# A decoder layer on one core: start loads in quarters, merge residuals from PSUM, residual scaling moved to the down projection

## The chip, the cores and the metric

The kernel runs on one core of a Trainium2 chip. The metric is the device time of one execution in microseconds (us), the median of several runs. The engines are named as the profile names them: PE (TensorE, matrix products; PEld is its weight load), DVE (VectorE), ACT (ScalarE), POOL (GpSimd) and SP (SyncE, which here only issues transfers).

## The reference, cut to what matters

One layer of a hybrid decoder on 544 rows (512 of a prompt and 8 sequences of 4) with 1024 channels and a feed-forward width of 2816. In the code below, attention, the convolution and the caches are left out.

```python
def token_mixers(u, mw, slopes, conv_prev, kv_prev):
    a = u @ w_in + b_in
    glu = a[..., :CONV_CH] * jax.nn.sigmoid(a[..., CONV_CH:QKV_OFF])
    qkv = a[..., QKV_OFF:GATE_OFF].reshape(B, T, 3, N_GROUPS, N_SLOTS, HEAD_DIM)
    gate_c = jax.nn.sigmoid(a[..., GATE_OFF:GATE_OFF + D_MODEL])
    gate_a = jax.nn.sigmoid(a[..., GATE_OFF + D_MODEL:])
    ...
    y_conv = conv_branch(conv_in, w_dw, b_dw, conv_ln_g, conv_ln_b, w_pc, b_pc)
    ...
    y_att = o.reshape(B, T, ATT_WIDTH) @ w_pa + b_pa
    y = (gate_c * y_conv + gate_a * y_att) @ w_out + b_out
    return y, new_kv, new_conv

def block(x, c, lw, slopes, conv_prev, kv_prev):
    ...
    mod = (jax.nn.silu(c) @ w_ada + b_ada)[:, None, :]
    sh1, sc1, g1, sh2, sc2, g2 = jnp.split(mod, 6, axis=-1)
    u = x * (1 + sc1) + sh1
    y, new_kv, new_conv = token_mixers(u, ..., slopes, conv_prev, kv_prev)
    x = layer_norm(DN_ALPHA * x + (1 + g1) * y, ln1_g, ln1_b)
    u = x * (1 + sc2) + sh2
    h = (jax.nn.silu(u @ w_gate) * (u @ w_up)) @ w_down
    x = layer_norm(DN_ALPHA * x + (1 + g2) * h, ln2_g, ln2_b)
    return x, new_kv, new_conv
```

## The kernel before, in words

All activations lie transposed, channels on the 128 partitions and rows along the free dimension, in two halves of 272 columns: h = 0 holds prompt rows 0 to 271, h = 1 the other 240 and the 32 sample rows. Each float32 product is made of three products of a rounded high part and a low residual (high by high, high by low, low by high). So an operand has to be prepared: ACT casts it to the high part (L133, L828, L962) and DVE subtracts that from the original to get the residual (L134, L829, L952).

Weights come in blocks of 1024 x 128 through a stream: `load_more` issues loads on SP's queue into four buffers (`wr`), `prep_to(n)` prepares blocks up to number n, and `w_next` prepares up to three ahead and returns one. A buffer is loaded anew only when its block is prepared. `mm_group` (L199, L200, L202) multiplies one block with both halves: 48 products of 272 columns for eight row tiles. On PE, ACT, DVE and POOL the instructions run in the order in which the program writes them; background work is cut into generators that `tick` advances between groups of products.

**Start.** The modulation vector's first third is made in four groups g: `ada_mm(g)` is 32 products with a 2 MB weight tile `ga[g]` (64 entries in the trace), and `make_u(g)` copies the result, transposes it on PE, makes `modT` on DVE (it needs the `vec` load) and from it the rows of tiles 2g and 2g + 1 of the modulated input `U`. The first three blocks of the input projection accumulate as tiles come (`early_mm(g)`, 36 products each); the loop from the fourth block on uses `mm_group`. The other two thirds of the modulation run between later blocks (`ada_gen`), from eight 2 MB loads (`ada_load`) on POOL's queue.

**Merge and output projection.** For each of eight channel tiles the attention projection is added on POOL (L845) to the gated convolution branch, and `merge_split` makes the operand rows `M`. The output projection (weights `wo`) then takes half 0 for all eight blocks, and half 1 after it. `z` is loaded again with the input rows, scaled by ALPHA with a bias on POOL (L989), and takes each block's result. `Stats` gathers the sums for the layer norm: a running sum on DVE (L881), squares on ACT (L873) added on POOL (L882), each turned into column sums by PE with a matrix of ones (L924, L925); `finish` makes the mean and the deviation. `ln1_gen(h)` normalizes and makes the feed-forward input `u2[h]`; for half 0 it also keeps its float32 rows in `TF` (L976), during half 1's projection.

**Feed-forward.** Gate and up blocks run in three chunks. Blocks 0 to 3 run classically, blocks 4 to 20 by `seven`: seven products of half-size operands in place of eight, with sums of weights made on POOL (L1077) and sums of rows (`T`) made from `tf` on DVE (L1262 to L1267). In the first chunk `keep` multiplies the rows of `z` by ALPHA and the norm's gain (L1258), a few rows at a time between the blocks. The chunk ends with a down projection whose results are added to `z`.

## Time and profile before

| | us |
|---|---|
| median of 3 runs | 1032.31 |
| lowest, highest | 1032.12, 1032.55 |
| profiled execution | 1033.35 |
| its span | 1031.6 |
| mean granted clock of PE in it | 0.986 of full speed |

A row of a timeline gives the start and the duration of one instruction, or of a run of equal ones (xN, with their time together), and in brackets how long the engine stood idle before it and what ended that. Tables of stretches give the busy time of each engine in a stretch, with the instructions that touch it. The granted clock is 1.00 at 2.4 GHz and 0.50 at 1.2 GHz.

### The profile page before, as it was taken

Reading aid. Unit: us, or ns where it says so; the run is one execution under the profiler, and the core shown is the slowest. Engines: PE = TensorE matmul, PEld = TensorE weight load, DVE = VectorE, ACT = ScalarE, POOL = GpSimd, SP = SyncE. Lnnn points to the kernel's source line nnn. Section 1 sums busy time; section 2 is a strip of 40 time slices with the busy share of each in tenths; the row PEclk is TensorE's granted clock in tenths of the full one; section 3 lists DMA queues with packets and bytes.
Section 4 is the critical chain, followed back from the end, with each engine's and each line's share of the span. In section 5 each row is a group of like instructions: output and inputs, shape, how many; then the busy total and the mean of one; then the engine's idle time right before and its main releaser. Section 6 shows DMA issues by size and latency. Waiting matters only on the chain.

```text
span 1031.6 us, 21539 instructions
## 1 busy us (share of the span) xinstructions
PE 985.8 (96%) x8964; PEld 942.2 (91%) x8964; DVE 652.1 (63%) x1156; ACT 479.7 (47%) x931; POOL 236.3 (23%) x279
## 2 busy tenths in 40 slices
PE   4999999999999999999999998989999999999995
PEld 3887999999998999999999998989999999999994
DVE  3422788879886654342217887687546875578687
ACT  3312235545447667534433445656325652266333
POOL 0301010010013310101103444054014440344046
PEclk8999999999999999999999998999999999999998
DMA  9998687696784674699953620124964769565612
GB/s 379 361 385 319 244 298 261 246 339 233 277 324 163 238 271 154 236 378 384 367 202 99 242 83 21 42 83 170 349 255 162 266 209 360 205 246 207 213 50 86
DMA packets 44945, 242.64 MB, mean 235 GB/s; under 512 B 7408, under 2 KB 10736, under 8 KB 37680
## 3 DMA queue, kind: packets, MB, share of 16 engines
q1 hardware_dynamic: 34592, 126.83, 34.4%
q10 hardware_dynamic: 7632, 88.43, 23.0%
q0 software_dynamic: 2624, 26.02, 6.3%
q8 instruction: 70, 1.15, 0.4%
q14 instruction: 27, 0.22, 0.1%
HBM read 231.36 MB, written 97.58 MB: 319 GB/s over the span
## 4 chain that ended last, share of the span: by engine, by line
PE 61%; DVE 12%; issue 8%; ACT 7%; POOL 6%; DMA 5%; ACTq 0%; DVEq 0%; POOLq 0%
PE mm L199 15%; PE mm L200 14%; PE mm L202 14%; POOL ss L1077 4%; DMA wr<-in_w_gu 3%; PE od L740 2%; PE mm L1120 2%; PE Sd L705 2%; PE mm L1121 2%; PE mm L1122 2%; PE adaps L334 1%; DVE mrg L829 1%; DMA wr<-in_w_in 1%; PE pt L516 1%; DVE wl L134 1%
## 5 line engine op out<-in xcount | busy, mean ns | idle before, releaser
L199 PE MATMUL mm<-u,wh 128*128 128x272 f32 x1016 | 283.4, 296 | 1.2 <-ACT wh L133 0.9
L200 PE MATMUL mm<-u,wh 128*128 128x272 f32 x1016 | 275.6, 289 | 0.0
L202 PE MATMUL mm<-u,wl 128*128 128x272 f32 x1016 | 213.2, 290 | 1.3 <-DVE wl L134 1.2
L199 PEld LDWEIGHTS mm<-u,wh 128*128 128x128 f32 x1016 | 192.4, 189 | 15.8 <-issue 11.4
L200 PEld LDWEIGHTS mm<-u,wh 128*128 128x128 f32 x1016 | 192.7, 190 | 0.3
L134 DVE TENSOR_TENSOR wl<-wr,wh 128x1024 fp32r<-128x1024 f32 (+2 forms) x100 | 117.5, 1176 | 86.5 <-ACT wh L133 86.5
L202 PEld LDWEIGHTS mm<-u,wl 128*128 128x128 f32 x1016 | 160.4, 189 | 1.9 <-DVE wl L134 1.9
L133 ACT CAST wh<-wr 128x1024 fp32r<-128x1024 f32 (+2 forms) x100 | 97.0, 972 | 64.6 <-PE mm L200 50.5
L439 DVE SCALAR_TENSOR_TENSOR convy<-glu,vec,convy 128x512 f32<-128x512 f32 x120 | 95.7, 797 | 2.5
L1077 POOL TENSOR_TENSOR ss<-wr 128x512 f32<-128x512 f32 x34 | 50.6, 1487 | 189.3 <-DVE s L1104 85.9
L200 PE MATMUL mm<-h,wh 128*128 128x272 f32 x240 | 64.7, 288 | 0.0
L199 PE MATMUL mm<-h,wh 128*128 128x272 f32 x240 | 64.5, 286 | 0.0
L1034 DVE SCALAR_TENSOR_TENSOR z<-mm,modT,z 128x272 f32<-128x272 f32 (+1 forms) x48 | 21.7, 479 | 49.0 <-PE mm L202 49.0
L637 ACT ACTIVATE qk<-mm,vec 128x272 f32<-128x272 f32 (+1 forms) x48 | 25.9, 627 | 56.5 <-PE mm L202 56.5
L202 PE MATMUL mm<-h,wl 128*128 128x272 f32 x240 | 49.6, 288 | 0.0
L1093 ACT CAST wh<-ss 128x512 fp32r<-128x512 f32 (+1 forms) x34 | 28.4, 835 | 42.8 <-POOL ss L1077 32.1
L199 PEld LDWEIGHTS mm<-h,wh 128*128 128x128 f32 x240 | 45.2, 188 | 0.0
L200 PEld LDWEIGHTS mm<-h,wh 128*128 128x128 f32 x240 | 45.1, 188 | 0.0
L1120 PE MATMUL mm<-ta,wh 128*128 128x272 f32 x136 | 40.4, 297 | 4.6 <-DVE wg L1142 4.6
L509 ACT ACTIVATE P<-P,st 128x256 f32<-128x256 f32 x64 | 31.2, 488 | 28.2 <-DVE st L503 25.7
L654 POOL DMA_DIRECT2D out_kv<-qk x4 | 2.4, 597 | 182.5 <-ACT qk L637 182.5
L200 PE MATMUL mm<-mrg,wo 128*128 128x272 f32 x128 | 37.8, 296 | 1.8 <-DVE mrg L829 1.7
(329 smaller groups left out, 2545.4 us busy)
## 6 DMA issues: line engine op xcount, KB each, us to landing
out_s<-in_c ACTq DMA_DIRECT2D x32, 2044.0 KB, 10.4
wr<-in_w_in SPq DMA_DIRECT2D x60, 512.0 KB, 6.6
wr<-in_w_gu SPq DMA_DIRECT2D x44, 512.0 KB, 3.8
KT<-in_kt SPq DMA_DIRECT2D x24, 792.0 KB, 7.9
VV<-in_vv SPq DMA_DIRECT2D x24, 768.0 KB, 7.8
gb<-in_w_ada POOLq DMA_DIRECT2D x8, 2048.0 KB, 16.9
out_s<-in_c ACTq DMA_DIRECT2D x8, 2032.0 KB, 10.1
ga<-in_w_ada SPq DMA_DIRECT2D x8, 1024.0 KB, 14.3
```

The source lines that it names most:

```text
L133: act.copy(out=hv, in_=raw)
L134: dve.tensor_tensor(out=lv, in0=raw, in1=hv.bitcast(F32), op=ALU.subtract)
L199: pe.matmul(ps[h][:, :HC], lhsT=hi[:, k], rhs=A[h][:, 0, k], start=(k == 0), stop=False)
L200: pe.matmul(ps[h][:, :HC], lhsT=hi[:, k], rhs=A[h][:, 1, k], start=False, stop=False)
L202: pe.matmul(ps[h][:, :HC], lhsT=lo[:, k], rhs=A[h][:, 0, k], start=False, stop=(k == nk - 1))
L439: dve.scalar_tensor_tensor(out=o, in0=src, scalar=sc, in1=o, op0=ALU.mult, op1=ALU.add)
L509: act.activation(out=p[:, a:b], in_=p[:, a:b], func=AF.Exp, bias=st[:, kd, s, hh, 0:1], accum_out=st[:, kd, s, hh, 1:2])
L637: act.activation(out=o, in_=src, func=AF.Identity, bias=V("b_in", col))
L1034: dve.scalar_tensor_tensor(out=zz[:, :n1], in0=ps[:, :n1], scalar=modT[:, 5, m, 0:1], in1=zz[:, :n1], op0=ALU.mult, op1=ALU.add)
L1077: pool.tensor_tensor(out=o, in0=x, in1=y, op=op)
L1093: act.copy(out=hi, in_=src_of(f, n))
L1120: pe.matmul(ps[:, :HC], lhsT=hi[:, k], rhs=B[:, 0, k], start=(first and k == 0), stop=False, skip_group_check=not first)
```

## The change

At the start, the x tiles and the first three weight blocks are loaded in quarters, one set behind each modulation group, and prepared in quarters (`prep_quarters`). The products of the first three blocks are spread differently over the groups, and 18 products of a matrix of ones (`warm`) are added. The large constant load and four of the modulation loads are issued on SP's queue in place of ACT's and POOL's. In the merge, ACT copies the high part to PSUM as well, and the residual reads that copy in seven of eight tiles. The first two output blocks run interleaved, rows 0 to 5 of both ahead of rows 6 and 7. ACT in place of POOL scales `z`. `finish` writes POOL's additions first and the reciprocal ahead of the second pair. The float32 rows of `u2[0]` are made in the feed-forward start (`again`) in place of the second half's projection, and the second up block is prepared there. `keep` moves to the first chunk's down projection.

```diff
@@ -214,16 +214,26 @@
     act.dma_start(out=vec, in_=I["vec"])
-    ga = []
-    for g in range(4):
-        t = big_tile(3 + g, [128, 8, 512], F32, f"ga{g}")
+    ga = [big_tile(3 + g, [128, 8, 512], F32, f"ga{g}") for g in range(4)]
+
+    def ga_load(g):
         for i in range(2):
-            sp.dma_start(out=t[:, 4 * i:4 * i + 4], in_=I["w_ada0"][g, :, 4 * i:4 * i + 4])
-        if g % 2 == 0:
-            sp.dma_start(out=x_sb[:, 2 * g:2 * g + 4], in_=I["x_t"][:, 2 * g:2 * g + 4])
-        if g < 2:
-            load_more(1 + 2 * g)
-        ga.append(t)
+            sp.dma_start(out=ga[g][:, 4 * i:4 * i + 4], in_=I["w_ada0"][g, :, 4 * i:4 * i + 4])
+
+    def x_load(g):
+        sp.dma_start(out=x_sb[:, 2 * g:2 * g + 2], in_=I["x_t"][:, 2 * g:2 * g + 2])
+
+    def w_quarters(g):
+        for m in range(NE):
+            sp.dma_start(out=eraw[m][:, 2 * g:2 * g + 2], in_=stream[m][0][:, 2 * g:2 * g + 2])
+
+    NE = 3
+    eraw = [wrp.tile([128, 8, 128], F32, tag="wr", name="wr") for _ in range(NE)]
+    for g in range(4):
+        ga_load(g)
+        x_load(g)
+        w_quarters(g)
+    pos.update(load=NE, prep=NE, use=NE)
     load_more()
-    act.dma_start(out=cst[:, 128:], in_=I["cst"][:, 128:])
-    dve.memset(cpad, 0.0)
+    sp.dma_start(out=cst[:, 128:], in_=I["cst"][:, 128:])
     dve.memset(ones, 1.0)
+    dve.memset(cpad, 0.0)
     dve.memset(epst, EPS)
@@ -282,9 +292,23 @@
 
-    NE = 3
     early = [[(pmm if m < 2 else ps_s).tile([128, 512], F32, tag="mm" if m < 2 else "s", name="mm") for _ in range(2)] for m in range(NE)]
-    ew = []
 
-    def early_mm(g):
+    def warm(n):
+        t = ps_t.tile([128, 128], F32, tag="t", name="warm")
+        for _ in range(n):
+            pe.matmul(t, lhsT=ones, rhs=ones, start=True, stop=True)
+
+    ew = [(whp.tile([128, 8, 128], F32R, tag="wh", name="wh"), wlp.tile([128, 8, 128], F32R, tag="wl", name="wl")) for _ in range(NE)]
+
+    def prep_quarters(g):
+        ks = slice(2 * g, 2 * g + 2)
         for m in range(NE):
             hi, lo = ew[m]
+            act.copy(out=hi[:, ks], in_=eraw[m][:, ks])
+            dve.tensor_tensor(out=lo[:, ks], in0=eraw[m][:, ks], in1=hi[:, ks].bitcast(F32), op=ALU.subtract)
+            done[m] = g == 3
+        load_more()
+
+    def early_mm(g, ms=range(NE)):
+        for m in ms:
+            hi, lo = ew[m]
             for k in (2 * g, 2 * g + 1):
@@ -297,19 +321,18 @@
 
-    a0 = ada_mm(0)
-    make_u(0, a0)
-    prep_to(1)
-    a1 = ada_mm(1)
-    prep_to(2)
-    make_u(1, a1)
-    prep_to(3)
-    for m in range(NE):
-        ew.append(preps.pop(m))
-    pos["use"] = NE
-    early_mm(0)
-    a2 = ada_mm(2)
-    make_u(2, a2)
-    early_mm(1)
-    a3 = ada_mm(3)
-    make_u(3, a3)
-    early_mm(2)
+    warm(12)
+    make_u(0, ada_mm(0))
+    prep_quarters(0)
+    warm(6)
+    early_mm(0, (0, 1))
+    make_u(1, ada_mm(1))
+    prep_quarters(1)
+    early_mm(0, (2,))
+    early_mm(1, (0,))
+    make_u(2, ada_mm(2))
+    prep_quarters(2)
+    early_mm(1, (1, 2))
+    early_mm(2, (0,))
+    make_u(3, ada_mm(3))
+    prep_quarters(3)
+    early_mm(2, (1, 2))
     dve.tensor_scalar(out=qb, in0=V("b_in", 0, 60), scalar1=0.125, scalar2=None, op0=ALU.mult)
@@ -320,5 +343,5 @@
 
-    def ada_load(c):
+    def ada_load(c, eng=pool):
         t = big_tile(aslots[c], [128, 2, 2048], F32, f"gb{c}")
-        pool.dma_start(out=t, in_=I["w_ada12"][c])
+        eng.dma_start(out=t, in_=I["w_ada12"][c])
         abox[c] = t
@@ -364,4 +387,4 @@
     ctmp = glu[:, 4 * 542 + 4 * NB * 34:].rearrange("p (b t w) -> p b t w", b=NB, w=CW)
-    for c in range(4):
-        ada_load(c)
+    for c in range(2):
+        ada_load(c, sp)
     pool.memset(glu_p[:, :, 0:30], 0.0)
@@ -397,3 +420,6 @@
         glu_evict(m, ps)
-        next(ada12, None)
+        if m > NE:
+            next(ada12, None)
+        if m < NE + 2:
+            ada_load(m - NE + 2, sp)
     pool.dma_start(out=O["conv_s"], in_=glu_s.rearrange("p c b t -> p (c b t)"))
@@ -827,4 +853,9 @@
     def merge_split(m, mg, h):
+        hi = M[h][:, 0, m].bitcast(F32)
         act.copy(out=M[h][:, 0, m], in_=mg[:, h * HC:(h + 1) * HC])
-        dve.tensor_tensor(out=M[h][:, 1, m], in0=mg[:, h * HC:(h + 1) * HC], in1=M[h][:, 0, m].bitcast(F32), op=ALU.subtract)
+        if m < DM:
+            seen = ps_s.tile([128, 512], F32, tag="s", name="mhi")[:, :HC]
+            act.copy(out=seen, in_=hi)
+            hi = seen
+        dve.tensor_tensor(out=M[h][:, 1, m], in0=mg[:, h * HC:(h + 1) * HC], in1=hi, op=ALU.subtract)
 
@@ -932,7 +963,9 @@
             ndb = nd.unsqueeze(1).to_broadcast([128, 2, HC])
-            for k in pairs:
-                dve.tensor_tensor(out=self.zt(k, 2), in0=self.zt(k, 2), in1=ndb, op=ALU.add)
             for k in range(2 * len(pairs), 8):
                 pool.tensor_tensor(out=self.zt(k), in0=self.zt(k), in1=nd, op=ALU.add)
+            for k in pairs[:1]:
+                dve.tensor_tensor(out=self.zt(k, 2), in0=self.zt(k, 2), in1=ndb, op=ALU.add)
             dve.reciprocal(out=sd, in_=sd)
+            for k in pairs[1:]:
+                dve.tensor_tensor(out=self.zt(k, 2), in0=self.zt(k, 2), in1=ndb, op=ALU.add)
             return sd
@@ -969,9 +1002,2 @@
         u2[h] = A
-        if h == 0:
-            yield
-            for k in range(8):
-                if k % 2 == 0:
-                    yield
-                zk = stats.zt(k)
-                act.activation(out=TF[0][:, k // 4, k % 4], in_=zk, func=AF.Identity, scale=G9[:, k, 0:1], bias=B9[:, k, 0:1])
 
@@ -981,12 +1007,21 @@
         for m in range(8):
-            if h == 0:
+            if h == 0 and m == 0:
+                wo.extend((w_next(), w_next()))
+                pair = [pmm.tile([128, 512], F32, tag="mm", name="mm") for _ in range(2)]
+                for ks in (range(6), (6, 7)):
+                    for i in range(2):
+                        for k in ks:
+                            pe.matmul(pair[i][:, :HC], lhsT=wo[i][0][:, k], rhs=M[0][:, 0, k], start=(k == 0), stop=False)
+                            pe.matmul(pair[i][:, :HC], lhsT=wo[i][0][:, k], rhs=M[0][:, 1, k], start=False, stop=False)
+                            pe.matmul(pair[i][:, :HC], lhsT=wo[i][1][:, k], rhs=M[0][:, 0, k], start=False, stop=(k == 7))
+            elif h == 0 and m > 1:
                 wo.append(w_next())
-            ps = mm_group(wo[m], M, 8, halves=(h,))[h]
+            ps = pair[m] if h == 0 and m < 2 else mm_group(wo[m], M, 8, halves=(h,))[h]
             n1 = HC if h == 0 else 240
             zz = stats.zt(m)
-            if h == 0 and m == 0:
-                for k in range(8):
-                    pool.tensor_scalar(out=z[:, k, :NP], in0=z[:, k, :NP], scalar1=ALPHA, scalar2=xbb[:, k:k + 1], op0=ALU.mult, op1=ALU.add)
-                prep_to(pos["use"] + XP)
-                pool.tensor_scalar(out=z[:, :, NP:], in0=z[:, :, NP:], scalar1=ALPHA, scalar2=None, op0=ALU.mult)
+            if h == 0 and m < 7:
+                for k in ((0, 1) if m == 0 else (m + 1,)):
+                    act.activation(out=z[:, k, :NP], in_=z[:, k, :NP], func=AF.Identity, scale=ALPHA, bias=xbb[:, k:k + 1])
+            if h == 0 and m == 6:
+                act.activation(out=z[:, :, NP:], in_=z[:, :, NP:], func=AF.Copy, scale=ALPHA)
             dve.scalar_tensor_tensor(out=zz[:, :n1], in0=ps[:, :n1], scalar=modT[:, 2, m, 0:1], in1=zz[:, :n1],
@@ -1251,14 +1286,13 @@
 
-            keeps = [(k, h) for h in range(2) for k in range(8)]
-
-            def keep(n):
-                for _ in range(min(n, len(keeps))):
-                    k, h = keeps.pop(0)
-                    zk = z[:, k, h * HC:(h + 1) * HC]
-                    act.activation(out=zk, in_=zk, func=AF.Identity, scale=agb[:, 0, k:k + 1], bias=agb[:, 1, k:k + 1])
-
-            for i in range(2):
-                gu_evict({0: first[2 * i]}, {0: first[2 * i + 1]}, H, i)
+            def again(ks):
+                for k in ks:
+                    act.activation(out=tf[:, k // 4, k % 4], in_=z[:, k, :HC], func=AF.Identity, scale=G9[:, k, 0:1], bias=B9[:, k, 0:1])
+
+            gu_evict({0: first[0]}, {0: first[1]}, H, 0)
+            again(range(4))
+            gu_evict({0: first[2]}, {0: first[3]}, H, 1)
             dve.tensor_tensor(out=tf[:, 0], in0=tf[:, 2], in1=tf[:, 0], op=ALU.subtract)
             act.copy(out=T["S1"][:, 0], in_=tf[:, 0])
+            again(range(4, 8))
+            prep_to(pos["use"] + 2)
             dve.tensor_tensor(out=t3, in0=tf[:, 3], in1=tf[:, 2], op=ALU.subtract)
@@ -1267,3 +1301,2 @@
             dve.tensor_tensor(out=t4, in0=tf[:, 1], in1=tf[:, 3], op=ALU.subtract)
-            keep(4)
             A = u2[1]
@@ -1284,3 +1317,2 @@
             dve.tensor_tensor(out=T["S2"][:, 1], in0=tf[:, 3], in1=f32(T["S2"][:, 0]), op=ALU.subtract)
-            keep(2)
             up_evict(sg, pu, H, 2)
@@ -1303,3 +1335,2 @@
             own["S4"] = one.tile([128, 2, 4, 128], F32R, tag="osb", name="s4")
-            keep(2)
             pu = mm_group(w_next(1), u2, 8)
@@ -1315,4 +1346,2 @@
             seven(f, f - k0, H, f + 1 in wg, hooks)
-            if j == 0:
-                keep(2)
             copies(0.8)
@@ -1329,4 +1358,14 @@
             flush()
+
+            def keep(m):
+                for h in range(2):
+                    zk = z[:, m, h * HC:(h + 1) * HC]
+                    act.activation(out=zk, in_=zk, func=AF.Identity, scale=agb[:, 0, m:m + 1], bias=agb[:, 1, m:m + 1])
+
+            if j == 0:
+                keep(0)
             for m in range(8):
                 ps = mm_group(w_next(), H, nf)
+                if j == 0 and m < 7:
+                    keep(m + 1)
                 for h in range(2):
```

## Rows read from the trace of the kernel before

**Rows 1.** The page: part 1 (busy us, share, instructions) and part 6 (issues to landing).

```profile
PE 985.8 (96%) x8964; PEld 942.2 (91%) x8964; DVE 652.1 (63%) x1156; ACT 479.7 (47%) x931; POOL 236.3 (23%) x279
...
wr<-in_w_gu SPq DMA_DIRECT2D x44, 512.0 KB, 3.8
```

**Rows 2.** Table of stretches: busy by engine, granted clock, DMA share, GB/s.

```profile
core 0: us, PE busy (x) PEld busy (x) DVE busy (x) ACT busy (x) POOL busy (x), PEclk, DMA share, GB/s
10.00:20.00 10.00, 3.29 (x53) 2.61 (x57) 4.27 (x10) 3.42 (x7) 0.66 (x2) 0.64 1.01 415
...
80.00:90.00 10.00, 10.00 (x82) 8.39 (x81) 3.80 (x9) 2.02 (x3) 1.52 (x3) 1.00 1.00 415
575.90:579.30 3.40, 3.40 (x18) 3.40 (x17) 2.58 (x3) 3.40 (x5) 1.41 (x1) 0.51 1.00 390
580.00:590.00 10.00, 10.00 (x80) 9.92 (x79) 7.98 (x12) 1.06 (x1) 7.80 (x8) 1.00 0.74 264
```

**Rows 3.** Timeline of the start: start us, us, engine, line, work, [idle <-releaser].

```profile
6.51 3.44 PE L256 MATMUL adaps<-ga,cpad 128*32 128x128 f32 x64 [6.51 <-DVE cpad L233]
...
10.35 0.33 PE L264 MATMUL modt<-cst,modsb 128*128 128x128 f32 x1 [0.40 <-ACT modsb L262]
11.84 0.26 DVE L267 SCALAR_TENSOR_TENSOR modT<-modt,vec 128x18 f32<-128x18 f32 x2 [5.38 <-DMA vec<-in_vec]
...
14.25 1.04 ACT L133 CAST wh<-wr 128x1024 fp32r<-128x1024 f32 x1
...
16.57 1.94 PE L256 MATMUL adaps<-ga,cpad 128*32 128x128 f32 x32 [5.89 <-DMA ga<-in_w_ada]
...
35.59 1.95 PE L256 MATMUL adaps<-ga,cpad 128*32 128x128 f32 x64
...
40.63 0.23 ACT L246 CAST u<-us 128x64 fp32r<-128x64 f32 x1
...
41.42 0.22 DVE L247 TENSOR_TENSOR u<-us,u 128x64 fp32r<-128x64 f32 x1
...
47.20 0.29 PE L199 MATMUL mm<-u,wh 128*128 128x272 f32 x1
```

**Rows 4.** Timeline, DVE and PE, from the merge into the output projection.

```profile
569.80 1.96 DVE L829 TENSOR_TENSOR mrg<-mg,mrg 128x272 fp32r<-128x272 f32 x2
...
574.19 0.39 PE L200 MATMUL mm<-mrg,wo 128*128 128x272 f32 x1 [1.73 <-DVE mrg L829]
...
576.21 0.44 DVE L829 TENSOR_TENSOR mrg<-mg,mrg 128x272 fp32r<-128x272 f32 x1 [0.48 <-ACT mrg L828]
```

**Rows 5.** Timeline of POOL at the first output projection.

```profile
577.89 9.07 POOL L989 TENSOR_SCALAR z<-z,xbb 128x512 f32<-128x512 f32 x8 [6.43 <-DMA z<-in_x_t]
```

**Rows 6.** Timeline, ACT, DVE and PE, at the end of the second half's projection.

```profile
630.25 3.13 ACT L976 ACTIVATE tf<-z,B,G 128x272 f32<-128x272 f32 x6
...
631.89 0.44 DVE L881 TENSOR_TENSOR lns<-lns,z 128x272 f32<-128x272 f32 x1
...
634.65 1.27 PE L925 MATMUL lnps<-lnq,ones 128*128 128x272 f32 x2 [1.54 <-POOL lnq L882]
```

**Rows 7.** Timeline, DVE, ACT and PE, in the first feed-forward blocks.

```profile
656.42 1.28 DVE L1264 TENSOR_TENSOR t<-tf 128x1088 f32<-128x1088 f32 x1
...
660.08 2.13 ACT L1258 ACTIVATE z<-z,agb 128x272 f32<-128x272 f32 x4
...
663.17 1.23 DVE L134 TENSOR_TENSOR wl<-wr,wh 128x1024 fp32r<-128x1024 f32 x1 [2.81 <-ACT wh L133]
...
669.50 1.23 DVE L134 TENSOR_TENSOR wl<-wr,wh 128x1024 fp32r<-128x1024 f32 x1 [0.50 <-ACT wh L133]
...
693.33 0.39 PE L1120 MATMUL mm<-ta,wh 128*128 128x272 f32 x1 [2.18 <-DVE wg L1142]
...
699.33 0.44 DVE L1142 TENSOR_TENSOR wg<-wg,c 128x272 f32<-128x272 f32 x1 [0.86 <-ACT wg L1206]
...
705.06 0.39 PE L1120 MATMUL mm<-ta,wh 128*128 128x272 f32 x1 [0.88 <-DVE wg L1142]
```

More of the change, by code (lines that the diff above doesn't have):

```diff
@@ L214, in hybrid_step_kernel @@
     act.dma_start(out=vec, in_=I["vec"])
-    ga = []
-    for g in range(4):
-        t = big_tile(3 + g, [128, 8, 512], F32, f"ga{g}")
-        for i in range(2):
-            sp.dma_start(out=t[:, 4 * i:4 * i + 4], in_=I["w_ada0"][g, :, 4 * i:4 * i + 4])
-        if g % 2 == 0:
-            sp.dma_start(out=x_sb[:, 2 * g:2 * g + 4], in_=I["x_t"][:, 2 * g:2 * g + 4])
-        if g < 2:
-            load_more(1 + 2 * g)
-        ga.append(t)
+    ga = [big_tile(3 + g, [128, 8, 512], F32, f"ga{g}") for g in range(4)]
[9 more added lines that the diff above has]
+    eraw = [wrp.tile([128, 8, 128], F32, tag="wr", name="wr") for _ in range(NE)]
+    for g in range(4):
+        ga_load(g)
+        x_load(g)
+        w_quarters(g)
+    pos.update(load=NE, prep=NE, use=NE)
     load_more()
-    act.dma_start(out=cst[:, 128:], in_=I["cst"][:, 128:])
+    sp.dma_start(out=cst[:, 128:], in_=I["cst"][:, 128:])
+    dve.memset(ones, 1.0)
     dve.memset(cpad, 0.0)
-    dve.memset(ones, 1.0)
     dve.memset(epst, EPS)
@@ L981, in hybrid_step_kernel @@
         for m in range(8):
-            if h == 0:
+            if h == 0 and m == 0:
+                wo.extend((w_next(), w_next()))
+                pair = [pmm.tile([128, 512], F32, tag="mm", name="mm") for _ in range(2)]
+                for ks in (range(6), (6, 7)):
+                    for i in range(2):
+                        for k in ks:
[3 more added lines that the diff above has]
+            elif h == 0 and m > 1:
                 wo.append(w_next())
-            ps = mm_group(wo[m], M, 8, halves=(h,))[h]
+            ps = pair[m] if h == 0 and m < 2 else mm_group(wo[m], M, 8, halves=(h,))[h]
             n1 = HC if h == 0 else 240
             zz = stats.zt(m)
-            if h == 0 and m == 0:
-                for k in range(8):
-                    pool.tensor_scalar(out=z[:, k, :NP], in0=z[:, k, :NP], scalar1=ALPHA, scalar2=xbb[:, k:k + 1], op0=ALU.mult, op1=ALU.add)
-                prep_to(pos["use"] + XP)
-                pool.tensor_scalar(out=z[:, :, NP:], in0=z[:, :, NP:], scalar1=ALPHA, scalar2=None, op0=ALU.mult)
+            if h == 0 and m < 7:
[3 more added lines that the diff above has]
+                act.activation(out=z[:, :, NP:], in_=z[:, :, NP:], func=AF.Copy, scale=ALPHA)
             dve.scalar_tensor_tensor(out=zz[:, :n1], in0=ps[:, :n1], scalar=modT[:, 2, m, 0:1], in1=zz[:, :n1],
@@ L1250, in hybrid_step_kernel @@
             prep_to(pos["use"] + 1)
-            keeps = [(k, h) for h in range(2) for k in range(8)]
-            def keep(n):
-                for _ in range(min(n, len(keeps))):
-                    k, h = keeps.pop(0)
-                    zk = z[:, k, h * HC:(h + 1) * HC]
-                    act.activation(out=zk, in_=zk, func=AF.Identity, scale=agb[:, 0, k:k + 1], bias=agb[:, 1, k:k + 1])
-            for i in range(2):
-                gu_evict({0: first[2 * i]}, {0: first[2 * i + 1]}, H, i)
+            def again(ks):
[4 more added lines that the diff above has]
+            gu_evict({0: first[2]}, {0: first[3]}, H, 1)
             dve.tensor_tensor(out=tf[:, 0], in0=tf[:, 2], in1=tf[:, 0], op=ALU.subtract)
             act.copy(out=T["S1"][:, 0], in_=tf[:, 0])
+            again(range(4, 8))
+            prep_to(pos["use"] + 2)
             dve.tensor_tensor(out=t3, in0=tf[:, 3], in1=tf[:, 2], op=ALU.subtract)
```

## Prediction

> **What bounds the kernel now.** I read the page's first part, then a table of stretches, then PE alone in order of time for its gaps, and last the other engines around each gap. PE is busy 96% of the span [rows 1], and in its full stretches a 272-column product starts every 0.122 us (82 in 10 us) [rows 2]. So time can come only from the few places where PE waits or runs at half clock. The reader is to see four. (a) The start: the fourth block's first product is at 47.20 [rows 3], though the work up to there is 144 early products (17.6 us) and four modulation products of 1.95 (7.8). (b) The first output projection, where PE waits 1.73 for a DVE residual [rows 4] and then runs at half clock [rows 2]. (c) The end of the second half's projection, where the sum of squares comes 1.54 late [rows 6]. (d) The first feed-forward blocks, where PE waits 2.18, 0.88 and (the second's repetition one block on) 0.90 for PSUM banks that DVE frees late [rows 7]. Elsewhere PE is the bound, and what other engines save is worth nothing.
>
> **Start.** Before, the first three weight blocks come whole, and the products of group g run behind the modulation product of g+1. After, the blocks come in quarters, and one or two blocks of group g run just ahead of that product. I add up the chain that this makes. From the end of a modulation product (35.59 + 1.95 = 37.54) ACT is through with its u rows at 40.63 + 0.23 = 40.86, 3.32 later, and DVE at 41.42 + 0.22 = 41.64, 4.10 later [rows 3]. Then come the weight quarters, 256 wide, which the trace doesn't show: bounds are the 64-wide pair (0.23, 0.22) and the 1024-wide pair (1.04, 1.23) [rows 3, 7]; I take the line between them, 0.39 on ACT and 0.42 on DVE. First residual: 4.10 + 0.42 = 4.52. Of a block's 12 products four go ahead of it and eight after: 4.52 + 8 x 0.122 = 5.5, with a handover 5.55; two blocks 7.0, three 8.5. So the first modulation product ends at 6.51 + 3.44 = 9.95, the second at 9.95 + 7.0 + 1.95 = 18.9, the third at 18.9 + 5.55 + 1.95 = 26.4, the fourth at 33.9, and the early blocks at 33.9 + 8.5 = 42.4. Against 47.20 that is 4.8 earlier.
>
> What could spoil it? The vec load, which holds the first group until 11.84, has half an x load (0.56 MB) less ahead of it: at 415 GB/s [rows 2] 1.35 earlier, 10.5, and the transposed product that it joins ends at 10.35 + 0.33 [rows 3], so that wait goes. The fourth modulation weights come behind 11.5 MB in all (8.4 of their own kind, three x pieces, nine quarters, 0.25 of small loads): at 415 GB/s from 2 us that is 30, wanted at 33.9 - 1.95 = 31.9. The loads are just hidden, and what they lose beyond 2 us counts in full. Last, the clock: it reads 0.64 over 10 to 20 us [rows 2], with a pause of PE of 5.89 in it [rows 3]. The 18 added warm products fill part of the pauses, but some 1.5 us stay in each group. At the lower level a product starts every 0.21 us (18 in 3.4 us, two of them cut by the edges [rows 2]); the 24 products of the first group would lose 2.1, of which I take 0.9. **Start: -3.9, bounds -5 to 0.**
>
> The Trainium skill speaks against the quarters: DMA: Bandwidth & Descriptors, section Anatomy of one DMA, gives a transfer a fixed cost of about 2 us beside its bytes, by which I estimate 2.3 us for a quarter of 128 KB, and nine of them one after the other would put 18 us ahead of the fourth group. The trace speaks for overlap: 415 GB/s over 10 to 20 us from a queue that holds several transfers.
>
> The modulation loads that move from POOL's queue to SP's stand there behind three weight refills, which wait for the last quarter's residual at about 33.9 + 5.4 = 39.3. With 1.6 MB of refills ahead of 2.1 MB, 9 us, the first is in at 49; it is wanted after the fifth block, at 42.4 + 2 x 5.9 = 54. The eighth weight block, behind two of these loads, comes near 57, and its own product starts at 72. Cost 0; without that cover 1 to 2 us.
>
> **Merge and first projection.** The residual takes 0.98 while POOL adds and 0.44 without [rows 4]. With one operand in PSUM it may no longer collide (bounds 0.44 and 0.98); ACT pays 14 copies of about 0.4 (the quarter's price), two to a block of 2.9 us of PE. Beside that, the first two output blocks run 36 products ahead of rows 6 and 7, 4.4 us of cover in place of 2.2, and the gap was 1.73. Either edit alone covers it. Gone with it is the half clock behind it: 3.4 us for about 16 products, 3.4 - 16 x 0.122 = 1.4 [rows 2]. The scaling of z moves from POOL (eight in 9.07 us) to ACT [rows 5], which is busy 1.06 of 10 us there [rows 2]. **-3.1, bounds -1.7 to -3.6.**
>
> **Second half's norm and feed-forward start.** Six rows on ACT from 630.25 to 633.38 stand ahead of the last square, whose input is there at 631.89 [rows 6]. With them moved, the square and POOL's add end 1.4 earlier and the 1.54 wait all but goes: PE gains 1.4 there, perhaps more if the clock holds. The chain to the second half's rows starts 1.3 earlier. But the eight rows come back on ACT in the feed-forward start, at 3.13 / 6 = 0.52 each, 4.2. They are in the path: DVE begins the second half's gates behind a weight residual (663.17) that waited 2.81 for ACT, and ACT had four scalings of 2.13 ahead of it [rows 7]. After: -1.3 (earlier start) + 4.2 (rows) - 2.1 (scalings gone to the down projection) + 1.3 (a subtraction that was covered and now follows the residual) + 0.5 (a sigmoid, priced as a row, that follows too) = +2.6; I take 2.4. Queued behind are the next gate block's weights (DVE at 669.50 [rows 7], just in time for PE now): they come 2.4 late, PE loses its gain in one wait of some 4 us, and all up to the bank wait at 693.33 moves by +2.4. Behind that, two scalings in each of four blocks are what DVE waits 0.86 for at 699.33 [rows 7]; without them the 0.88 and its repetition go, -1.8. In the down projection the 16 scalings, 0.53 each, two to a block of 5.9 us, are covered by PE; uncovered they would be 8. **+0.6, bounds -3.5 (rows fit into ACT's waits, PE keeps its gain) to +3.** The reordered norm (POOL's adds first, the reciprocal before the second pair) trades places on DVE: 0 to -0.3, taken as 0.
>
> **Sum.** -3.9 - 3.1 + 0.6 = -6.4. The profiled execution took 1033.35 (span 1031.6 and 1.75 around it), so 1026.95; it stands 1.04 over the median of 1032.31, so 1025.9 for the median.
>
> **Rivals.**
> A, the feed-forward rows are free, and PE keeps 3.5 there. For it: ACT often waits for DVE between a gate's sigmoid and its cast. Against: ACT is in order, and a row placed behind the cast fills no such wait. 1032.3 - 3.9 - 3.1 - 3.5 = 1021.8.
> B, the clock stays low through the first two groups: 2.1 + 1.1 of the 4.8 lost, start -1.6, time 1028.2; with part of the third group 1029.5. For it: the 1.73 pause before 574.19 was enough for the low level.
> C, the new wait of 4 us in the feed-forward start brings the low level too: 24 products x 0.09 = 2.1 more, 1028. For it, what follows 574.19; against, PE waits for DVE behind it anyway (693.33).
> D, slower: all four groups run at the lower level. On the path that adds 2.1 + 1.0 + 2.1 + 4.6 = 9.8, the start ends at 52.2, 5.0 late: 5.0 - 3.1 + 0.6 = +2.5, 1034.8. It decides from 7.3 us of added time on, some 80 of the 144 products. Against it: the low reading now goes with one pause of 5.89, and the new pauses are of 1.5.
> E, slower: the quarters don't overlap. A 512 KB load lands in 3.8 us [rows 1], 1.26 of it bytes at 415 GB/s; the other 2.5 paid nine times puts the fourth group at 30 + 22, the start's end at 61.5 and the time at 1044. It decides from 0.8 us or so for each quarter. Against it, the full queue in rows 2. The page named above is the one from which it would follow.
> F, the change doesn't do what it says: B and C together eat the gain, 1031 to 1032.5.
>
> **Numbers.** Forecast 0.46 (1023.7 to 1027.5), A 0.17, B 0.13, C 0.12, F 0.04, D 0.05, E 0.03. A measurement of this kernel tells 0.2%, 2 us, from no change. Faster (forecast, A, B, C): 0.88; same (F): 0.04; slower (D, E): 0.08. The range, 1020.8 to 1030.5, leaves out D, E, F and an edge of A.
>
> **What would show it.** Start: the fourth block's first product at 42.4 to 44, the granted clock in each stretch up to there, a wait for the fourth modulation weights (E). Projection: no gap over 0.3 us and clock 1.00 in the ten us behind the last attention block; residuals near 0.45. Norm: no wait on POOL for the sum of squares. Feed-forward: a new wait of 3 to 4 us for the weights of the fourth gate block, and none for banks in the second and third block of seven products. I am wrong if the start is bound by loads, if the clock falls in it, or if ACT hides the eight rows.

## The result, and the profile of the changed kernel

The changed kernel takes 1027.22 us (median of 4 runs, 1026.28 to 1027.54); the kernel before takes 1032.43 beside it. The ratio is 0.9937 with a 95% interval of 0.9922 to 0.9952: 5.2 us less at the medians, 6.5 by the ratio (5.0 to 8.1 by its interval). The forecast was 1025.9, range 1020.8 to 1030.5. The profiled execution took 1026.28 (span 1024.5, before 1031.6).

I read it in the order of the four places. First PE at the start, in order of time, as in [rows 3]:

```profile
8.63 1.08 PE L266 MATMUL adaps<-ga,cpad 128*32 128x128 f32 x32 [0.93 <-DMA ga<-in_w_ada]
11.11 1.57 PE L298 MATMUL warm<-ones 128*128 128x128 f32 x12 [0.69 <-DVE modT L277]
17.09 1.95 PE L266 MATMUL adaps<-ga,cpad 128*32 128x128 f32 x64
...
42.89 0.29 PE L199 MATMUL mm<-u,wh 128*128 128x272 f32 x1
...
79.56 1.92 PE L357 MATMUL adaps<-gb,cpad 128*32 128x512 f32 x16 [0.34 <-DMA gb<-in_w_ada]
```

The fourth block's first product stands at 42.89, 4.31 earlier than before. The last row is new: PE waits 0.34 for a modulation load that now stands in SP's queue. Then the loads (KB each, median us from issue to landing, in the first 45 us):

```profile
ga<-in_w_ada SPq DMA_DIRECT2D x8, 1024.0 KB, 8.9
...
wr<-in_w_in SPq DMA_DIRECT2D x5, 512.0 KB, 8.1
...
wr<-in_w_in SPq DMA_DIRECT2D x12, 128.0 KB, 8.3
```

Then stretches, to be held against [rows 2]: the start, and the eight us in which the output projection begins.

```profile
10.00:20.00 10.00, 7.95 (x106) 6.99 (x107) 4.25 (x14) 3.43 (x10) 0.66 (x2) 1.00 1.04 406
...
569.00:573.00 4.00, 3.85 (x30) 3.64 (x30) 2.97 (x5) 3.15 (x5) 0.00 (x0) 1.00 0.99 399
573.00:577.00 4.00, 4.00 (x34) 4.00 (x33) 2.19 (x5) 2.46 (x4) 0.00 (x0) 1.00 1.02 407
```

The granted clock (third figure from the right) is 1.00 where it was 0.64 at the start and 0.51 behind the merge, and behind the merge PE has no gap over 0.2. The merge's residual on DVE and the copy on ACT that it reads, grouped by line (ns: least, median, most):

```profile
L860 DVE TENSOR_TENSOR mrg<-mg,mhi x14: 422/430/439, 548.8 to 568.1; 128x272 fp32r<-128x272 f32 x14
```

```profile
L858 ACT COPY mhi<-mrg x14: 390/390/392, 548.2 to 567.2; 128x272 f32<-128x272 f32 x14
```

The residual is 0.43 all fourteen times, and the copy that pays for it on ACT 0.39. Next the second half's norm, PE's waits, which answer to [rows 6]:

```profile
624.99 0.73 PE L955 MATMUL lnps<-lns,ones 128*128 128x272 f32 x2 [1.71 <-DVE lns L912]
...
625.94 0.73 PE L956 MATMUL lnps<-lnq,ones 128*128 128x272 f32 x2 [0.23 <-POOL lnq L913]
```

The 1.54 for the sum of squares is 0.23. The first row's products in the kernel before:

```profile
632.39 0.72 PE L924 MATMUL lnps<-lns,ones 128*128 128x272 f32 x2 [1.72 <-DVE lns L881]
```

So the changed kernel has a lead of 7.40 there (it stands that much earlier). At the second row the lead is 8.71, and it grows further, because the kernel before runs its next products at the lower level. A stretch behind these rows, first before, then in the changed kernel:

```profile
634.00:638.00 4.00, 3.35 (x13) 3.11 (x14) 3.19 (x4) 1.73 (x4) 3.31 (x4) 0.50 0.29 45
```

```profile
628.00:632.00 4.00, 4.00 (x34) 4.00 (x33) 3.77 (x5) 0.62 (x2) 2.84 (x5) 1.00 0.41 131
```

The feed-forward start, by engine (ACT, DVE, PE), against [rows 7]:

```profile
643.78 2.13 ACT L1289 ACTIVATE tf<-z,B,G 128x272 f32<-128x272 f32 x4
...
650.43 2.12 ACT L1289 ACTIVATE tf<-z,B,G 128x272 f32<-128x272 f32 x4
652.46 1.03 ACT L133 CAST wh<-wr 128x1024 fp32r<-128x1024 f32 x1
```

```profile
653.52 1.23 DVE L134 TENSOR_TENSOR wl<-wr,wh 128x1024 fp32r<-128x1024 f32 x1 [4.19 <-ACT wh L133]
```

```profile
653.54 0.40 PE L199 MATMUL mm<-u,wh 128*128 128x272 f32 x1 [2.29 <-ACT wh L133]
654.80 0.52 PE L202 MATMUL mm<-u,wl 128*128 128x272 f32 x2 [0.49 <-DVE wl L134]
...
663.94 0.39 PE L199 MATMUL mm<-u,wh 128*128 128x272 f32 x1 [1.83 <-ACT wh L133]
665.20 0.65 PE L202 MATMUL mm<-u,wl 128*128 128x272 f32 x2 [0.49 <-DVE wl L134]
...
687.75 0.39 PE L1155 MATMUL mm<-ta,wh 128*128 128x272 f32 x1 [1.65 <-DVE wg L1177]
...
698.81 0.39 PE L1155 MATMUL mm<-ta,wh 128*128 128x272 f32 x1 [0.22 <-DVE wg L1177]
```

The reader should see one chain: four u2 rows on ACT (650.43), behind them the high part of the third up block's weights (652.46), behind that the residual on DVE, which idled 4.19, and PE, which waits 2.29 + 0.49 there and 1.83 + 0.49 for the fourth gate block. PE waited for the third up block in the kernel before too, but for less:

```profile
663.19 0.39 PE L199 MATMUL mm<-u,wh 128*128 128x272 f32 x1 [0.93 <-ACT wh L133]
```

Where this wait begins the lead is 11.0 (662.26 before, 651.25 now). The first bank wait (PE waits for a PSUM bank that DVE frees late) ended at 693.33 and ends at 687.75, a lead of 5.6: the feed-forward start takes 5.4, all that was won since the 7.40 and 1.8 more. The later bank waits give back 0.66 (0.88 is 0.22) and 0.90 (gone).

### The profile page after: what moved, and what is told of

It reads as the page before. It is cut to its first block, busy times and chain, and to the rows that moved or that the text cites. A ratio compares the mean times of both kernels' runs of the same rounds, so it can differ in the third digit from the quotient of the medians.

```text
span 1024.5 us, 21678 instructions
## 1 busy us (share of the span) xinstructions
PE 989.5 (97%) x9000; PEld 945.6 (92%) x9000; DVE 649.0 (63%) x1165; ACT 492.5 (48%) x963; POOL 223.8 (22%) x266
## 4 chain that ended last, share of the span: by engine, by line
PE 56%; DVE 13%; issue 10%; ACT 8%; DMA 7%; POOL 6%; ACTq 0%; SPq 0%; POOLq 0%; DVEq 0%
PE mm L199 13%; PE mm L200 13%; PE mm L202 13%; POOL ss L1112 4%; DMA gb<-in_w_ada 3%; DMA wr<-in_w_gu 2%; PE od L766 2%; PE mm L1155 2%; PE Sd L731 2%; PE mm L1157 2%; PE mm L1156 2%; DVE wl L134 1%; PE pt L542 1%; DMA wr<-in_w_in 1%; PE adaps L357 1%
## 5 line engine op out<-in xcount | busy, mean ns | idle before, releaser
L133 ACT CAST wh<-wr 128x1024 fp32r<-128x1024 f32 (+2 forms) x97 | 94.0, 970 | 48.5 <-PE mm L200 34.6
L1157 PE MATMUL mm<-tb,wl 128*128 128x272 f32 x136 | 39.5, 290 | 0.0
```

The lines of the kernel that those rows point to most:

```text
L133: act.copy(out=hv, in_=raw)
L1157: pe.matmul(ps[:, :HC], lhsT=lo[:, k], rhs=B[:, 0, k], start=False, stop=(k == 3), skip_group_check=not first)
```

## The experiments

Medians of each kernel and ratios to the kernel before, which ran beside each (its medians 1032.43 for the first row and 1033.3 to 1033.5 for the others). Differences between two of these kernels are given at the medians; where their intervals overlap, the times alone do not tell them apart, and the reading rests on one trace of each:

| kernel | us | ratio, 95% interval |
|---|---|---|
| changed kernel | 1027.22 | 0.9937, 0.9922 to 0.9952 |
| start alone | 1029.40 | 0.9967, 0.9957 to 0.9977 |
| merge alone | 1029.82 | 0.9970, 0.9960 to 0.9979 |
| pair of blocks alone | 1032.91 | 1.0000, 0.9990 to 1.0009 |
| PSUM copy alone | 1030.73 | 0.9979, 0.9970 to 0.9989 |
| changed, no warm products | 1028.65 | 0.9958, 0.9942 to 0.9975 |
| changed, scalings back | 1030.44 | 0.9970, 0.9960 to 0.9980 |
| changed, rows back | 1024.74 | 0.9928, 0.9913 to 0.9943 |
| changed, rows back and spread | 1022.57 | 0.9904, 0.9889 to 0.9919 |
| changed, weights ahead of rows | 1025.12 | 0.9920, 0.9905 to 0.9934 |
| spread, weights earlier | 1021.37 | 0.9881, 0.9864 to 0.9897 |
| spread, two weights earlier | 1021.03 | 0.9880, 0.9866 to 0.9895 |
| changed, loads on POOL | 1027.90 | 0.9947, 0.9932 to 0.9962 |

**Start alone.** The diff's first six parts on the kernel before.

> The kernel before with the edits of the start alone (quartered weight blocks, warm products, products of the first blocks ahead of the next modulation product, modulation loads on SP's queue); the merge, the projection and the feed-forward are as before. Theory: the first product of the fourth block comes near 42.9 in place of 47.20, and as PE is the bound behind it nearly all of that reaches the end: -3.9 us (0.4 of 4.3 is given back by the changed order of loads, before 305 us). Rival 1: part of what the start gains is lost in the later waits, as those are set by DMA or by ACT and DVE: -2 us or less. Rival 2: the start's gain in the whole change came from somewhere else, 0.

3.4 us less (2.4 to 4.4): the theory, not rival 1. The small gap of PE that begins at 308.93 in the kernel before begins 3.7 earlier. It held a surprise, PE at the end of the merge and the stretches behind it:

```profile
570.48 0.39 PE L200 MATMUL mm<-mrg,wo 128*128 128x272 f32 x1 [1.72 <-DVE mrg L855]
```

```profile
570.40:574.40 4.00, 3.87 (x28) 3.65 (x29) 2.97 (x7) 2.48 (x5) 0.01 (x1) 1.00 0.90 353
574.40:578.40 4.00, 4.00 (x34) 4.00 (x33) 3.27 (x6) 1.86 (x2) 4.00 (x4) 1.00 1.05 428
```

The same pause of 1.72, to 0.01, and no lower level behind it: 34 products in 4 us at a granted clock of 1.00. So the 1.4 that the prediction charged to that pause in [rows 2, 4] belongs to it in one execution and not in another. At the norm's first column sums this kernel's lead is 4.8 (627.62 for 632.39), 1.1 more than at 308.93: that is what the lower level had cost the other execution up to there.

**Merge alone, and its two edits apart.** The merge's and the projection's parts on the kernel before, without the move of the rows:

```diff
+        if m < DM:
+            seen = ps_s.tile([128, 512], F32, tag="s", name="mhi")[:, :HC]
+            act.copy(out=seen, in_=hi)
+            hi = seen
...
+                for ks in (range(6), (6, 7)):
+                    for i in range(2):
+                        for k in ks:
...
+                    act.activation(out=z[:, k, :NP], in_=z[:, k, :NP], func=AF.Identity, scale=ALPHA, bias=xbb[:, k:k + 1])
```

The first of these edits is the copy, the second the pair. The third, ACT's scaling of `z`, ran only together with them.

> The kernel before with the edits of the merge and of the first projection alone (copy of the high part in PSUM, two output blocks ahead of rows 6 and 7, scaling of z on ACT); the start, the u2 rows and the feed-forward are as before. Theory: the gap of 1.73 at the end of the merge and the stretch at the lower clock behind it go, -3.5 us at the end of the projection, and the wait of 1.54 for the sum of squares and the bank waits in the feed-forward stay as they were: -3.5 us at the end. Rival 1: only the gap goes and the lower clock has another cause: -1.7. Rival 2: a later wait takes it back, as the second half's norm hangs on ACT and not on PE: the wait of 1.54 grows, -1 to -2.

3.1 us less (2.2 to 4.1): the theory.

> The kernel before with one edit of the merge alone: the first two output blocks are computed as a pair, rows 0 to 5 of both ahead of rows 6 and 7. No copy in PSUM; the scaling of z stays on POOL. Theory (as the prediction has it, either edit covers the gap): PE has 4.4 us of products in place of 2.2 ahead of the late residual, the wait of 1.73 goes and with it the lower clock: -3.1 to -3.5 us, as both edits together. Rival: the residual at 0.98 is later than that for more than the last row, a wait of 0.5 to 1 stays and brings the lower clock with it: -1 or less.

> The kernel before with the other edit of the merge alone: the high part is copied to PSUM, and the residual reads it there. No pair of blocks; the scaling of z stays on POOL. Theory (as the prediction has it): with 14 residuals at 0.43 in place of up to 0.98 the last one comes about 2 us earlier, the wait of 1.73 goes and with it the lower clock: -3.1 to -3.5 us. Rival: the chain of the last row (sum on POOL, high part on ACT, copy on ACT, residual on DVE) sets the wait, the copy adds 0.4 to it, and a wait of 1 us or more stays: 0 to -1.

The two part ways. The pair alone is not told from the kernel before; the copy alone gives 2.2 us (1.1 to 3.1). That is less than its theory and more than its rival, and it is not told from all three edits together: at the norm's first column sums the two kernels stand 0.4 apart (629.41 and 629.00). With the pair the wait for the residual does go, and three others stand in its place on PE:

```profile
574.40 0.39 PE L990 MATMUL mm<-mrg,wo 128*128 128x272 f32 x1 [0.36 <-DVE wo L134]
...
578.63 0.39 PE L199 MATMUL mm<-mrg,wo 128*128 128x272 f32 x1 [0.43 <-ACT wo L133]
...
579.89 0.40 PE L202 MATMUL mm<-mrg,wo 128*128 128x272 f32 x1 [0.74 <-DVE wo L134]
```

That is 1.53 for 1.73. The pair uses the second block's weights a block sooner and the third's as soon, but DVE, which makes their residuals, still comes late from the merge's slow ones (it starts three weight residuals in a row at 578.61). The copy works where the lateness is made, on DVE. Its rows in the copy's kernel:

```profile
559.69 1.32 DVE L134 TENSOR_TENSOR wl<-wr,wh 128x512 fp32r<-128x512 f32 x1
...
561.84 0.77 DVE L834 TENSOR_TENSOR mrg<-mg,mhi 128x272 fp32r<-128x272 f32 x2
```

Two residuals take 0.77 where two took 1.96 beside POOL [rows 4], while the weight residual, 0.68 before at this place, now falls under POOL's addition and takes 1.32. DVE still ends its last residual 1.9 earlier, and PE has no gap over 0.2 there.

**Without the warm products.**

```diff
-    warm(12)
-    warm(6)
```

> The changed kernel without its 18 warm products (12 ahead of the first modulation product, 6 ahead of the first early products). Theory: they hold the clock; without them the granted clock falls below 0.8 in the stretch from 8 to 16 us, the first modulation product takes 3.4 as before and the 24 products of the first group lose up to 2.1: the first product of the fourth block at 44 to 45.3 in place of 42.89, and 1.2 to 2.4 us slower at the end. Rival: the pauses are short enough by the new order alone, the clock reads 1.00 without them, and the time is that of the changed kernel within 0.3.

The fourth block's first product comes at 45.18, 2.3 later in the trace, and the time is 1.4 longer at the medians, with intervals that overlap. That is the theory's size, but not by the row that it named. The stretch with the first group's products, without the warm ones and then in the changed kernel:

```profile
14.00:18.00 4.00, 3.77 (x16) 3.77 (x17) 1.66 (x6) 0.79 (x3) 0.00 (x0) 1.00 1.01 390
```

```profile
14.00:17.00 3.00, 3.00 (x23) 2.75 (x21) 0.99 (x3) 0.12 (x1) 0.00 (x0) 1.00 0.98 396
```

16 products in 3.77 us, one every 0.23, against 23 in 3.00, with a granted clock of 1.00 in both records. The pause of PE ahead of them was 2.90; with the warm products 0.88. The step from one product to the next shows the lower pace, the clock's column here does not.

**The scalings back in the feed-forward** (4, 2, 2 and 2 a block, as before).

> The changed kernel with the 16 scalings put back from the down projection into the feed-forward start and the blocks of seven products (4, 2, 2 and 2 a block), as before; the eight u2 rows stay in the feed-forward start. Theory: the bank waits of the second and third block of seven come back (+0.7 and +0.9), and the four scalings ahead of the second half's gates put another 2.1 on ACT's chain to the fourth gate block's weights: +3 to +4 us, 1030 to 1031. Rival: ACT waits for DVE there anyway and hides them, +0 to +0.5.

3.2 us slower than the changed kernel, with intervals that do not meet: the theory's size, by a path of its own. The four scalings and what waits for them (ACT, then PE):

```profile
658.62 2.13 ACT L1297 ACTIVATE z<-z,agb 128x272 f32<-128x272 f32 x4
```

```profile
666.25 0.59 PE L199 MATMUL mm<-u,wh 128*128 128x272 f32 x1 [5.36 <-ACT wh L133]
```

This one wait for the fourth gate block's weights is 5.36 where it was 1.83 + 0.49. Of the bank waits that the theory had come back, the second does not, and the third is 0.53 (at 713.57).

**The rows back, and spread.** The first kernel puts the eight rows back behind the first half's u2 and takes them out of the feed-forward; the second spreads them:

```diff
+        if h == 0:
+            for n, ks in enumerate((range(4), (4, 5), (6, 7))):
+                if n:
+                    yield
+                for k in ks:
+                    act.activation(out=TF[0][:, k // 4, k % 4], in_=stats.zt(k), func=AF.Identity, scale=G9[:, k, 0:1], bias=B9[:, k, 0:1])
...
-            again(range(4))
-            again(range(4, 8))
```

> The changed kernel with the eight u2 rows of the first half put back on ACT into the first projection of the second half, as before; the 16 scalings stay in the down projection. Theory: the rows cost more in the feed-forward start than their leaving saves in the norm. Put back, the wait of 1.54 for the sum of squares returns with the lower clock behind it, but the two waits of 2.30 and 1.84 with 0.49 each for weights go, and with the 16 scalings gone from ACT too the bank wait of 1.65 shrinks to under 0.5: some 4 us faster than the changed kernel, near 1023. Rival: DVE's and ACT's chain from the second half's norm to the banks is the bound there, so that PE's waits only change their place: within 1 us of the changed kernel, 1026 to 1028.

> As the run before it (rows back in the projection), but the eight rows are issued earlier and spread over ACT's idle stretches in that projection: four right behind the first half's u2, two a block later, two another block later, so that none stands ahead of the last square. Theory: the norm's wait for the sum of squares stays away and the clock stays high there, and the feed-forward start is free of the rows: another 1.5 to 3 us faster than the run before it, 1020 to 1022. Rival: the rows delay the squares or the shifts of the second half where they now stand, and the wait for the sum of squares comes back in full: the same time as the run before it.

Rows back: 2.5 us faster than the changed kernel at the medians, 0.9 by the ratios, with intervals that overlap; at best the theory's direction, not its 4, and the rival is not excluded. In its trace the wait of 1.53 for the sum of squares is there again, and the bank wait did not shrink (DVE, then PE):

```profile
651.24 1.23 DVE L134 TENSOR_TENSOR wl<-wr,wh 128x1024 fp32r<-128x1024 f32 x1 [2.12 <-ACT wh L133]
```

```profile
627.73 0.95 PE L956 MATMUL lnps<-lnq,ones 128*128 128x272 f32 x2 [1.53 <-POOL lnq L913]
...
685.46 0.40 PE L1162 MATMUL mm<-ta,wh 128*128 128x272 f32 x1 [2.18 <-DVE wg L1184]
```

DVE idles 2.12 where it idled 2.81 with the scalings in the way [rows 7]: these weights are now prepared ahead of three of DVE's four differences, and their high part stands on ACT behind a copy that waits for the first. Spread, the rows fill idle time of ACT ahead of the squares, and the sum of squares is not waited for (ACT, then PE):

```profile
616.16 2.12 ACT L1008 ACTIVATE tf<-z,B,G 128x272 f32<-128x272 f32 x4
...
618.84 1.10 ACT L1008 ACTIVATE tf<-z,B,G 128x272 f32<-128x272 f32 x2
...
620.81 1.11 ACT L1008 ACTIVATE tf<-z,B,G 128x272 f32<-128x272 f32 x2
```

```profile
626.08 0.72 PE L956 MATMUL lnps<-lnq,ones 128*128 128x272 f32 x2
...
683.67 0.39 PE L1161 MATMUL mm<-ta,wh 128*128 128x272 f32 x1 [0.83 <-DVE wg L1183]
```

1022.57: another 2.2 us, with intervals that overlap, and 4.7 under the changed kernel (3.4 by the ratios), with intervals that do not meet. The move of the rows into the feed-forward cost that much against a better place in the old stage.

**The order of preparation.** First the changed kernel with the third up block's weights ahead of the second four rows (the expectation, and the account of the change, call it the second up block), then the spread kernel with these weights ahead of the first difference too, then also the fourth gate block's ahead of the second half's evictions.

```diff
+            prep_to(pos["use"] + 2)
             again(range(4, 8))
-            prep_to(pos["use"] + 2)
```

> The changed kernel with one change of order in the feed-forward start: the second up block's weights (the third weight block made there) are prepared ahead of the second four u2 rows on ACT, not behind them. Theory: of the wait of 2.30 + 0.49 the four rows (2.12 on ACT) are the cause; the wait shrinks to under 0.9, DVE's idle 4.19 to about 2, the gates of the second half and the fourth gate block's weights come 2 us earlier, and the time falls by 1.5 to 2.1. Rival: the rows only take ACT from elsewhere, the subtraction that needs them (DVE, 1.28) comes later by as much, and the wait of 1.84 for the next weights grows by what the first lost: 0.

2.1 us faster than the changed kernel (1025.12): the theory's size, with intervals that overlap. Its path was half the rival's: the wait of 2.29 + 0.49 is gone entirely, that for the next weights grew from 1.83 + 0.49 to 3.35,

```profile
662.11 0.59 PE L199 MATMUL mm<-u,wh 128*128 128x272 f32 x1 [3.35 <-ACT wh L133]
```

so that 1.75 of 5.1 us of waits went, and the bank wait fell to 1.24.

> The kernel with spread rows and one change of order: the second up block's weights in the feed-forward start are prepared ahead of the first Strassen-like difference of u2 and its copy, not behind them. Theory: DVE waits about 2 us for that weights' high part, which stands on ACT behind a copy that waits for DVE's own difference; in the new order both engines work on, the second half's gates come 2 us earlier, the wait of 2.64 for the fourth gate block's weights shrinks to under 1, and the time falls by 1.5 to 2.1 to near 1020.5. Rival: the raw weights or their buffer come free only when PE has ended the products of the second half, so that the preparation waits in its new place and holds both engines: 0 or slower by up to 3.

> As the run before it, and the fourth gate block's weights are prepared ahead of the evictions of the second half's first two gate and up blocks, not behind them. Theory: what is left of the wait for these weights goes, the evictions move 1.2 us back, which costs nothing as their banks are not wanted soon: a further -0.3 to -1. Rival: the bank wait of 0.83 in the first block of seven products grows by what is gained, as DVE has the same work up to there: 0.

In the first of these DVE's idle time before these weights falls from 2.12 to 0.51, and PE's 2.64 for the fourth gate block to 1.04 + 0.49:

```profile
646.89 1.23 DVE L134 TENSOR_TENSOR wl<-wr,wh 128x1024 fp32r<-128x1024 f32 x1 [0.51 <-ACT wh L133]
```

```profile
658.52 0.39 PE L199 MATMUL mm<-u,wh 128*128 128x272 f32 x1 [1.04 <-ACT wh L133]
...
682.32 0.39 PE L1161 MATMUL mm<-ta,wh 128*128 128x272 f32 x1 [2.16 <-DVE wg L1183]
```

It is 1.2 us faster than the spread kernel, of 1.5 to 2.1 expected, with intervals that overlap. The bank wait grew from 0.83 to 2.16: behind the wait for these weights PE ran at a granted clock of 0.50 in the spread kernel (660 to 664 us) and at 1.00 in this one, so it now comes to that place sooner than DVE frees the bank. The second gives 0.3 more, which is not told from nothing. Its rival's path did not come, as the bank wait is 1.39 there; but PE waits 1.74 at 658.94 for the evictions that were moved back. 1021.03 is 6.2 under the changed kernel and 12.4 under the kernel before beside it.

**The modulation loads on POOL's queue again.**

> The changed kernel with the modulation loads of parts 1 and 2 back on POOL's queue, where the kernel before has them, with its order of the products that use them. Theory: the wait of 0.34 at 79 us and the later landing of the fifth weight block go, and the 0.4 that the start's gain loses before 305 us comes back: -0.3 to -0.5. Rival: from POOL's queue four loads of 1 MB start at once beside the last quarters and refills, and the weights of the fourth to sixth block come later: +1 to +2.

The wait at 79 us goes, as the theory says, but others come, on PE:

```profile
52.16 0.52 PE L202 MATMUL mm<-u,wl 128*128 128x272 f32 x2 [0.38 <-DVE wl L134]
...
60.12 0.36 PE L199 MATMUL mm<-u,wh 128*128 128x272 f32 x1 [0.32 <-DVE glu L406]
```

The place at 305.04 in the changed kernel comes at 306.13, and 0.16 of that is there at the fourth block already (43.05). The time, 1027.90, is not told from the changed kernel's; by the one trace of each SP's queue is the better place, by some 0.9.

## Why the prediction was right

The sum was -3.9 - 3.1 + 0.6 = -6.4; the measured change is -5.2 at the medians and -6.5 by the ratio. Measured along one trace against the other: the start -4.31, of which 0.4 is given back by 305 us; the projection -3.5; from the norm to the end +0.3 (lead 7.40 at 624.99, span 7.1 shorter). By the ratios the whole is -6.5 and the two stages alone are -3.4 and -3.1, which leaves the norm and the feed-forward at nothing, within some 2.

**Start.** The chain was right: modulation products end at 9.71, 19.04, 26.63 and 34.27 (9.95, 18.9, 26.4, 33.9 predicted). The clock took none of the 0.9 set aside for it, so rival B and D fall, and the run without warm products shows that they hold it. In its place the chain itself came 0.5 later (42.89 for 42.4). Some 0.3 of that, by estimate, is the step from product to product: the timelines show 0.126, where the prediction took 0.122 from a stretch that also held other products, and 68 of the early products stand on the chain. The cover that I gave the moved loads ("cost 0") was too thin by 0.34 us: this wait is new, and without warm products, where PE comes 2.3 later, it is absent and the place at 308.93 keeps the whole lead of 2.0. Rival E falls: the quarters land 8.3 us after issue as the 1 MB loads do in 8.9, so they overlap. The fixed cost per transfer that the Trainium skill gives (DMA: Bandwidth & Descriptors, Anatomy of one DMA), there for transfers that POOL (GpSimd) issues, may be in each of these 8.3 us. On SP's queue it is not paid one after the other.

**Merge.** Mechanism and size were right, one claim wrong: "Either edit alone covers it." It failed at the pair, whose cover I counted in PE's products against the residual alone; the weights of the blocks behind stand in the same queue on DVE. The copy does most of the work; what the pair and ACT's scaling of `z` add is not told. A residual with one input in PSUM takes 0.43 all fourteen times, also beside POOL's additions, where one with both inputs in SBUF takes 0.98. The Trainium skill (GPSIMD Engine Reference, Key points) names DVE instructions with two SBUF inputs among those that contend with POOL; the traces agree. The part of the price that I laid to the clock, 1.4 of 3.1, was found in the profiled execution of before, but is absent in another with the same pause. So some 1.1 of the -3.5 along the traces belongs to that execution, and the measured 3.1 of the merge alone can't be divided between pause and clock by these runs.

**Norm and feed-forward.** The 1.54 went (0.23), as predicted; the rows back in their old place bring it back (1.53), while the reordered norm ran only within the whole. The clock held behind it, and PE gained 3.6 there (7.40 to 11.0), not 1.4. The eight rows did cost PE all that it had gained: DVE's chain is 1.8 later at the bank wait, 2.4 predicted, and the scalings' leaving gave 0.66 + 0.90 behind it, 1.8 predicted. The sum for that chain is right in size and in part by luck: it puts one subtraction behind the weight residual, where the trace has three (654.66 to 658.6), and it leaves out an ACT cast that stood ahead of these weights (659.07 before) and now follows them (657.31). The step that came out otherwise is the new wait: not one of 4 us for the fourth gate block, but 2.78 for the third up block and 2.32 for the fourth gate block. PE already waited for the former in the kernel before, 0.93 + 0.49, a wait that the prediction did not list. Rival A falls, as these waits show. The mechanism of rival C did come; the stretches behind the two waits, in the changed kernel:

```profile
654.00:658.00 4.00, 3.51 (x18) 3.29 (x17) 3.93 (x4) 0.69 (x1) 0.00 (x0) 0.65 0.44 131
...
666.00:670.00 4.00, 4.00 (x24) 4.00 (x23) 3.30 (x7) 2.07 (x4) 0.00 (x0) 0.64 0.47 137
```

The granted clock is 0.65 and 0.64, but behind each PE waits for weights or banks all the same: with it the bank wait ends 1.8 late, less than the 2.4 predicted without it.

**What the sum hid.** Within the +0.6 stand large terms of both signs: the scalings' move is worth 3.2, the rows' move costs 4.7 against spreading them (3.4 by the ratios). The total was right while one of the edits in it was a loss against a place that neither kernel uses.

## What to carry to other kernels

Work moved off an engine's busy stretch should first look for idle time of that engine in the same stage, ahead of the instruction that was late; moved a stage further it may stand on a longer chain. Where two in-order engines pass work to and fro, put the preparation that needs neither ahead of the step that waits. An edit that gives the waiting engine more cover pays only if everything else it then needs comes from elsewhere than the late queue.

## What the runs showed of the hardware that was not expected

- A pause of 1.73 us on PE was followed by some 15 products at the lower level in one kernel, and a pause of 1.72 by none in the other, with the same instructions around it.
- Behind a pause of 2.90 products started every 0.23 us for four us while the record of the granted clock read 1.00.
- POOL's slowing of DVE moves to the next operation with two SBUF inputs: the merge's residuals fell from 0.98 to 0.43, and the weight residuals beside them rose from 0.68 to 1.32.
- The start is not the same in each execution: the third modulation product ended at 30.37 in the profile of before and at 31.93 in that of the pair alone, which has the same code up to there (the product took 1.95 in one and 2.80 in the other). Spans of single profiles carry this 1.5 us, and so does the start's gain of 4.31, which is read from one trace of each kernel.
